# Two mixture-of-experts layers: the first pair of experts gathered alone in float32, later pairs in twos, filler products, and an output projection that ends half by half

## The chip, the cores and the metric

The kernel runs on one core of a Trainium2 chip. The metric is the device time of one execution in microseconds (us). Three executions of the kernel before took 2075.39, 2079.44 and 2080.48 us; the median, 2079.44 us, is the time before.

## The reference, cut to what matters

The program is two transformer blocks over 256 tokens of width 1024, all in float32. The first block has two sublayer pairs: a mixer (stick-breaking attention, then retention) with an output projection and a layer norm, followed by a mixture of experts (MoE) with a layer norm. Only the passage from the mixer's output projection through layer norm and router into the experts matters here:

```
h = x * (1 + scale) + shift                     # the MoE's input, x is the layer norm's output
logits = h @ router_w + router_b                # 16 experts in 4 groups
sel_group = argmax over groups of the sum of the two best probabilities
top_val, top_idx = top 2 of the logits inside that group;  top_w = softmax(top_val)
combine = sum_k one_hot(top_idx_k) * top_w_k    # 256 x 16, two entries per row
for e in range(16):
    hidden = silu(h @ w_gate[e]) * (h @ w_up[e])            # 1024 -> 512
    out += combine[:, e:e+1] * (hidden @ w_down[e])         # 512 -> 1024
```

The kernel computes only the rows that go to an expert: up to 64 rows per expert are gathered (a matrix product with a 0/1 matrix), two experts ("a pair") share one 128-wide tile, and there are eight pairs. A fallback behind a branch handles experts with more than 64 rows; it was not entered in the profiled execution.

## The kernel before, in words

Work is written as a straight program; a scheduler then orders the instructions of each engine by a simulated timeline, in program order where several are ready, so a later instruction can fill a gap that the simulation sees. `issue_after(ins)` keeps an instruction behind another on the same engine's queue.

TensorE products come in two kinds. Float32 products (`mm` on float32 tiles) are issued as two passes, so one product shows as two instructions in the trace. Products on "split" data (a high and a low part in float32r, made by `split`, line 148: a copy on ScalarE, line 151, and a subtraction on VectorE, line 153) are single passes; `mm3` multiplies high and low parts in three of them.

- `proj_out` (line 427) is the mixers' output projection. For each pair `k2` of 128-row blocks it loads a weight tile, splits it, and runs 12 products for token half t=0 and 12 for t=1.
- `layer_norm` (line 304) treats token half 0 and then half 1: two multiplies (L314), a scale-and-add with a row sum (L316), ScalarE's mean, squares and variance (L320, L324, L327), an inverse square root on GpSimd (L330), and the normalization on VectorE (L335).
- `logits` (line 554) transposes the normalized rows, copies them out of PSUM and multiplies them with the router weights (16 columns); L578 makes `r_L`. `route` (line 581) selects experts in a chain of small VectorE operations (L589 to L653). Between them stand filler products on float32 (`warm`, line 172), whose result nobody uses. Three small products give each token its slot, `pos`; `hots` (line 656) compares `pos` with a ramp to make the 0/1 matrices (L660).
- `moe` (line 664) issues weight transfers of 1 MB from SyncE's queue (L680), 96 per layer, 12 per pair. Fifteen buffers (6 `w`, 6 `hl`, 3 of the 5 `a`) hold weights. `load()` is called 14 times before the split of the normalized rows `xh` and once behind it; the fifteenth uses the buffer that `xh` leaves. `moe_rest` reads the largest expert's count into registers (L821) and branches (L822) on all engines.
- `moe_gather` (line 765) gathers two pairs at once: 32 products on the split rows, modulation on ScalarE and VectorE, then for each pair two transposes and a small product that give `m_dT` and `m_sw`, needed only when the pair's output is scattered. It is called before the loop for pairs 0 and 1, and in the loop in iterations 1, 3 and 5.
- In the loop each pair runs gate and up products (16 steps; two experts side by side on halves of the array), SiLU and a multiply (L724, L725), transposes of the hidden rows (L187), down products (8 steps), and the scatter of the pair before.

Of the kernel before, what the change touches and what calls it, by code (L numbers as in the profile page):

```python
# [15 lines left out]
OP = mybir.AluOpType  # L16
# [27 lines left out]
LAG = 2  # L44
ATR = 4
# [9 lines left out]
class Net:  # L55
# [116 lines left out]
    def warm(self, src, n=1):  # L172
# [10 lines left out]
        for _ in range(n):  # L183
            self.mm(pt, self.ones, src, True, True)

# [153 lines left out]

    def behind(self):  # L340
# [86 lines left out]
    def proj_out(self, src, o, y, first=True, last=True, between={}):  # L427

        nkb = o[0].shape[1]
        W = src.rearrange("(k p) n -> p k n", p=P)  # L430
        for k2 in range(nkb // 2):
# [4 lines left out]
            for t in range(T):  # L436
                for kk in range(2):
                    k = k2 * 2 + kk
                    oh, ol = o[0][:, k, t * P:t * P + P], o[1][:, k, t * P:t * P + P]
                    for hf in range(2):  # L440
                        cs = slice(hf * 512, hf * 512 + 512)
                        self.mm3(y[t][hf], (oh, ol), (wh[:, kk, cs], wl[:, kk, cs]),
                                 first and k == 0, last and k == nkb - 1)
# [110 lines left out]
    def logits(self, xh):  # L554
# [20 lines left out]
        while late:  # L575
            product()
        L = self.wk.tile([P, T, 16], F32, name="r_L", bufs=1)
# [3 lines left out]
    def route(self, L):  # L581
# [56 lines left out]
        self.mm(pr[:, 1], self.stri, sel[:, 1], False, True)  # L638
        cnt = self.wk.tile([P, 17], I32, name="r_cnt", bufs=1)
# [3 lines left out]
        first = self.hots(0, pos)  # L643
# [12 lines left out]
    def hots(self, pr, pos):  # L656

        dt = self.t2(512, F32R).rearrange("p (t e s) -> p t e s", t=T, e=4)
        for t in range(T):
            self.nc.vector.tensor_tensor(dt[:, t], self.iota128[:, None, :CAP].to_broadcast([P, 4, CAP]),  # L660
                                         pos[:, t, 2 * pr:2 * pr + 4, None].to_broadcast([P, 4, CAP]), op=OP.is_equal)
        return [dt[:, t].rearrange("p e s -> p (e s)") for t in range(T)]

    def moe(self, i, xh, sc, sh):
# [21 lines left out]

        hl = [self.act8(F32R).rearrange("p (t d) -> p t d", t=T) for _ in range(2)]
        for t in range(T):
            self.split(hl[0][:, t], hl[1][:, t], xh[:, t])
        xh = hl  # L690
        load()
# [14 lines left out]
        first = self.moe_gather(xh, sc, sh, hot, cmb, 0)  # L706
        self.phase(f"moe{i}")
        one = self.wk.tile([P, 1], F32, name="m_one", bufs=1)
        nc.scalar.activation(one, cmb[:, 0, 0:1], AF.Silu)
        xg, dT, sw = first.pop(0)  # L710
        nxt, late = first, None
        for pr in range(8):
# [46 lines left out]
    def modulate_slots(self, eng, out, in_, sc, sh, k):  # L759
        if eng == "s":  # L760
            self.nc.scalar.activation(out, in_, AF.Identity, scale=sc[:, k:k + 1], bias=sh[:, k:k + 1])
        else:
            self.nc.vector.tensor_scalar(out, in_, sc[:, k:k + 1], sh[:, k:k + 1], op0=OP.mult, op1=OP.add)

    def moe_gather(self, xh, sc, sh, d, cmb, pr):


        nc = self.nc
        xg = [self.t4().rearrange("p (k s) -> p k s", k=KB) for _ in range(2)]
        for k2 in range(KB // 2):  # L770
# [3 lines left out]
            for q in range(2):  # L774
                for kk in range(2):
                    k = 2 * k2 + kk
                    self.modulate_slots("vs"[k2 % 2], xg[q][:, k], pg[:, kk, q * P:q * P + P], sc, sh, k)
        out = []
        for q in range(2):
            dT = self.wk.tile([P, T, 128], F32R, name="m_dT", bufs=3)  # L780
            sw = self.wk.tile([P, 1], F32, name="m_sw", bufs=3)
            pw = self.psum()
            dq = [d[t][:, q * P:q * P + P].bitcast(F32) for t in range(T)]
# [1085 lines left out]
```

## Time and profile before

| | |
|---|---|
| time before, median of 3 | 2079.44 us (2075.39 to 2080.48) |
| profiled execution, its own time | 2080.8 us |
| its span in the trace | 2079.0 us |
| mean granted TensorE clock | 0.977 |
| busy: TensorE products, weight loads, VectorE, ScalarE, GpSimd | 95%, 74%, 59%, 39%, 20% |

The span is the stretch from the first to the last instruction of the program; 1.8 us of the execution lie around it. A matmul's end is modelled, so starts are the safer numbers; a TensorE that shows as busy is not at its peak. The two MoE layers are at about 186 to 460 us and 690 to 957 us, each from the end of the mixer's projection to the start of the next layer norm.

### The profile page before, as it was taken

The page shows a single profiled execution, that of the slowest core. Times are in us where ns is not written, and L with a number is a line of the kernel's source. Part 1 is how long each engine was busy: PE and PEld are TensorE (multiplying, and loading weights), DVE is VectorE, ACT ScalarE, POOL GpSimd, SP SyncE. Part 2 cuts the span into 40 slices and gives each one's busy share as a digit, 9 for nine tenths or more (in the row PEclk, how much of TensorE's full clock was granted, in tenths as well). Part 3 has the DMA queues.
Part 4 walks back from the last instruction along what each step waited for, and adds up shares of the span by engine and source line. Part 5 has one row for each costly group of instructions (what it writes and reads, how often), then busy time and mean ns, then how long its engine had stood idle before and what let it go on. Part 6 is the DMA issues. An engine that isn't in the chain of part 4 may idle for free.

```text
span 2079.0 us, 31873 instructions
## 1 busy us (share of the span) xinstructions
PE 1970.1 (95%) x12566; PEld 1531.0 (74%) x12567; DVE 1218.3 (59%) x2489; ACT 801.3 (39%) x1254; POOL 417.7 (20%) x319
## 2 busy tenths in 40 slices
PE   6999999989999999997888999999999999999998
PEld 4977443339998844335766889999999998888886
DVE  3645321128885422115587569767999986555555
ACT  3444111124454211113333544555444444444444
POOL 1000000002332000000231144544665550000000
PEclk8999999999999899998998999999999999999999
DMA  9797799997875699996332361544554445555554
GB/s 388 270 407 269 293 395 392 395 384 252 312 266 178 241 370 394 396 391 257 132 132 72 131 238 35 161 151 143 171 193 145 153 153 191 186 190 192 189 189 149
DMA packets 155888, 496.09 MB, mean 239 GB/s; under 512 B 10177, under 2 KB 10593, under 8 KB 147153
## 3 DMA queue, kind: packets, MB, share of 16 engines
q1 hardware_dynamic: 152880, 483.42, 64.6%
q0 software_dynamic: 2848, 10.53, 1.4%
q8 instruction: 102, 1.67, 0.3%
q14 instruction: 58, 0.47, 0.1%
HBM read 486.30 MB, written 7.61 MB: 238 GB/s over the span
## 4 chain that ended last, share of the span: by engine, by line
PE 76%; DVE 8%; ACT 2%; issue 2%; DMA 1%; POOL 1%; POOLq 0%; SPq 0%; DVEq 0%; ACTq 0%
PE ps L163 45%; PE y L163 28%; PE y L1200 1%; PE ps L187 1%; DMA w<-moe_w_down 1%; DVE pair L1547 1%; DVE hl L153 1%; DVE et L1471 1%; DVE i L1448 0%; ACT hl L151 0%; POOL hl L160 0%; DVE ps L1193 0%; DVE pos L1459 0%; DVE v L1447 0%; DVE t L725 0%
## 5 line engine op out<-in xcount | busy, mean ns | idle before, releaser
L163 PE MATMUL ps<-hn,pair 128*128 128x256 f32 x3072 | 383.3, 285 | 4.2 <-DVE pair L1547 4.1
L163 PEld LDWEIGHTS ps<-hn,pair 128*128 128x128 f32 x3072 | 373.8, 192 | 5.4 <-DVE pair L1547 4.9
L163 PE MATMUL ps<-w,t 128*64 128x512 f32 x624 | 278.9, 598 | 7.7 <-ACT t L196 2.7
L163 PE MATMUL ps<-hl,t 128*64 128x512 f32 x624 | 279.7, 599 | 4.5 <-DVE t L194 3.1
L1547 POOL TENSOR_TENSOR pair<-raw,pair 128x640 fp32r<-128x640 f32 x128 | 235.9, 1851 | 157.0 <-ACT pair L1545 150.8
L151 ACT CAST hl<-w 128x2048 fp32r<-128x2048 f32 x79 | 150.4, 1903 | 137.0 <-PE ps L163 81.3
L153 DVE TENSOR_TENSOR pair<-raw,pair 128x1024 fp32r<-128x1024 f32 x128 | 156.8, 1225 | 67.2 <-ACT pair L151 67.2
L163 PE MATMUL y<-pair,tmp 128*128 128x512 f32 x768 | 189.7, 395 | 0.0
L163 PE MATMUL y<-pair,eT 128*128 128x512 f32 x768 | 186.5, 391 | 0.0
L163 PEld LDWEIGHTS y<-pair,tmp 128*128 128x128 f32 x768 | 144.4, 188 | 33.9
L163 PEld LDWEIGHTS ps<-w,t 128*64 128x64 f32 x624 | 82.4, 137 | 117.2 <-issue 106.8
L163 PEld LDWEIGHTS y<-pair,eT 128*128 128x128 f32 x768 | 144.2, 188 | 32.4
L1545 ACT CAST pair<-raw 128x1024 fp32r<-128x1024 f32 x128 | 134.2, 1051 | 65.1 <-PE ps L163 24.6
L153 DVE TENSOR_TENSOR hl<-w,hl 128x2048 fp32r<-128x2048 f32 x51 | 118.2, 2318 | 52.8 <-ACT hl L151 49.2
L151 ACT CAST pair<-raw 128x1024 fp32r<-128x1024 f32 x128 | 133.8, 1045 | 1.1 <-issue 1.1
L163 PEld LDWEIGHTS ps<-hl,t 128*64 128x64 f32 x624 | 81.6, 137 | 68.8 <-issue 62.1
L163 PE MATMUL ps<-hl,a 128*128 128x256 f32 x1008 | 130.3, 287 | 1.8 <-ACT hl L151 1.8
L330 POOL TENSOR_TENSOR ln_st<-ln_st,c_mhalf 128x1 f32<-128x1 f32 x8 | 7.9, 982 | 604.0 <-ACT ln_st L327 604.0
L163 PEld LDWEIGHTS ps<-hl,a 128*128 128x128 f32 x1008 | 124.0, 191 | 6.1 <-ACT hl L151 2.0
L725 DVE TENSOR_TENSOR t<-t,ps 128x512 f32<-128x512 f32 x16 | 11.0, 688 | 171.5 <-PE ps L163 171.5
L163 PEld LDWEIGHTS ps<-a,hl 128*128 128x128 f32 x864 | 106.4, 195 | 3.5 <-issue 1.6
L163 PE MATMUL ps<-a,hl 128*128 128x256 f32 x864 | 108.6, 287 | 0.3 <-DVE a L153 0.3
(427 smaller groups left out, 3012.5 us busy)
## 6 DMA issues: line engine op xcount, KB each, us to landing
raw<-peer_u SPq DMA_DIRECT2D x128, 512.0 KB, 3.5
raw<-peer_v SPq DMA_DIRECT2D x128, 512.0 KB, 3.3
w<-ada_w SPq DMA_DIRECT2D x35, 1024.0 KB, 8.3
w<-moe_w_down SPq DMA_DIRECT2D x28, 1024.0 KB, 14.3
hl<-moe_w_down SPq DMA_DIRECT2D x28, 1024.0 KB, 14.2
w<-moe_w_up SPq DMA_DIRECT2D x26, 1024.0 KB, 14.3
hl<-moe_w_up SPq DMA_DIRECT2D x26, 1024.0 KB, 14.3
w<-moe_w_gate SPq DMA_DIRECT2D x24, 1024.0 KB, 14.4
```

What stands on the lines that cost most here:

```text
L151: nc.scalar.copy(hi, src)
L153: nc.vector.tensor_tensor(lo, src, hi.bitcast(F32), op=OP.subtract)
L163: self.last_mm = self.nc.tensor.matmul(out, lhsT=lhsT, rhs=rhs, start=start, stop=stop, skip_group_check=True)
L187: self.nc.tensor.transpose(out, in_, self.ident[:in_.shape[0], :in_.shape[0]])
L330: nc.gpsimd.tensor_tensor(st[:, 3:4], st[:, 2:3], self.mhalf[:, 0:1], op=OP.pow)
L725: nc.vector.tensor_tensor(hid, hid, pu, op=OP.mult)
L1200: self.nc.tensor.matmul(py[32 * q:32 * q + 32, :S], lhsT=self.s5_ct[ct][:, 4 * i + q], rhs=ab[q % 2][:, x, ri], start=j == 0, stop=j == 3, ...
L1471: V.tensor_reduce(et[:, 0:2, h], oh.rearrange("p a k j -> p a j k"), axis=AX.X, op=OP.add)
L1545: nc.scalar.copy(up[:, 0], ur)
L1547: lo = eng.tensor_tensor(up[:, 1, ks], ur[:, ks], up[:, 0, ks].bitcast(F32), op=OP.subtract)
```

## The change

The parts, in the order in which they run:

1. `proj_out`: in a last call (`last`), the second-last block pair's weights are held, and the last two pairs are multiplied together: 24 products for half 0, then 24 for half 1.
2. `logits` gets three filler products behind its last product, `route` five behind the `pos` products.
3. `hots` makes 0/1 matrices of a chosen number of experts and type: two experts in float32 for the first pair, before it was four in float32r. The register load of the count is put behind it on VectorE's queue.
4. The split of `xh` and the fifteenth `load()` move from in front of `route` to behind the first pair's gather.
5. `first_gather` gathers pair 0 alone with 16 float32 products from the unsplit `xh`. Its `m_dT` and `m_sw` (`moe_slots`) are made behind the gate and up products of pair 0.
6. Later gathers run in iterations 0, 2, 4 (pairs 1-2, 3-4, 5-6) and 6 (pair 7; its 32 products still cover two pairs' columns, and one pair's are used).
7. The fallback behind the branch gathers from the unsplit rows too.

```diff
+FILL = {"L": 3, "pos": 5}
+GATHER = {0: (1, (0, 1)), 2: (3, (0, 1)), 4: (5, (0, 1)), 6: (6, (1,))}
...
+    def fill(self, src, n):
+        with self.tc.issue_after(self.last_mm.ins):
+            self.warm(src, n)
...
 proj_out:
+            for kk in range(2):
+                held[k2 * 2 + kk] = wh[:, kk], wl[:, kk]
+            if not (last and k2 == nkb // 2 - 2):
+                for t in range(T):
+                    with self.tc.issue_after(self.last_mm.ins) if t and len(held) > 2 else nullcontext():
+                        for k, (h, l) in held.items():
...
+                                self.mm3(y[t][hf], (oh, ol), (h[:, cs], l[:, cs]),
+                                         first and k == 0, last and k == nkb - 1)
+                held = {}
...
 logits:
+        self.fill(h.rearrange("p k s -> p (k s)"), FILL["L"])
 route:
+        self.fill(self.ones, FILL["pos"])
...
-        first = self.hots(0, pos)
+        first = self.hots(0, pos, 2, F32)
...
 moe:
-        for t in range(T):
-            self.split(hl[0][:, t], hl[1][:, t], xh[:, t])
-        xh = hl
-        load()
         cmb, pos, cnt, hot = self.route(L)
...
-        first = self.moe_gather(xh, sc, sh, hot, cmb, 0)
+        xg, got = self.first_gather(xh, sc, sh, hot)
+        with self.after(*got):
+            for t in range(T):
+                self.split(hl[0][:, t], hl[1][:, t], xh[:, t], 512)
+        xh, nxt, late = hl, [], None
+        load()
         for pr in range(8):
...
+            if pr == 0:
+                dT, sw = self.moe_slots(hot, cmb, 0)
             hid = self.t2()
...
-            if pr % 2 and pr + 1 < 8:
-                nxt = self.moe_gather(xh, sc, sh, self.hots(pr + 1, pos), cmb, pr + 1)
+            if pr in GATHER:
+                b, qs = GATHER[pr]
+                nxt = self.moe_gather(xh, sc, sh, self.hots(b, pos), cmb, b, qs)
...
+    def first_gather(self, x, sc, sh, d):
+        xg, last = self.t4().rearrange("p (k s) -> p k s", k=KB), [None, None]
+        for half in range(2):
+            pg = self.psum((P, 4, P))
+            for kk in range(4):
+                k = half * 4 + kk
+                for t in range(T):
+                    self.mm(pg[:, kk], x[:, t, k * P:k * P + P], d[t], t == 0, t == 1)
+            for kk in range(4):
+                k = half * 4 + kk
+                last[kk % 2] = self.modulate_slots("sv"[kk % 2], xg[:, k], pg[:, kk], sc, sh, k)
+        return xg, last
...
 moe_rest:
-        most = nc.values_load(cnt[0:1, 16:17], min_val=0, max_val=S)
+        with self.tc.issue_after(self.hot.ins):
+            most = nc.values_load(cnt[0:1, 16:17], min_val=0, max_val=S)
```

## Rows read from the trace of the kernel before

**Rows 1.** The page, part 4: the chain that ended last, by engine.

```profile
PE 76%; DVE 8%; ACT 2%; issue 2%; DMA 1%; POOL 1%; POOLq 0%; SPq 0%; DVEq 0%; ACTq 0%
```

**Rows 2.** Windows: stretch, length, busy us per engine, clock, DMA share, GB/s.

```profile
226.00:441.00 215.00, 204.93 (x966) 87.58 (x964) 39.21 (x82) 29.29 (x58) 0.00 (x0) 0.99 1.04 393
```

**Rows 3.** Waits of TensorE, second layer's loop: total us, times, longest.

```profile
PE ps L163 <- DMA w<-moe_w_down: 1.4, 2, 0.7
```

**Rows 4.** Timeline of SyncE's queue: start, us, transfer; first layer.

```profile
205.15 0.37 SPq L680 DMA_DIRECT2D a<-moe_w_gate  x1
224.37 0.38 SPq L680 DMA_DIRECT2D w<-moe_w_gate  x1
```

**Rows 5.** Timeline, first layer's loop: down products' neighbours in pairs 0 and 7.

```profile
235.53 0.66 PE L187 MATMUL ps<-c_pack,t 128*128 128x128 f32 x4 [0.89 <-DVE t L725]
...
444.63 0.64 PE L163 MATMUL ps<-w,t 128*64 128x512 f32 x1 [0.68 <-ACT t L196]
```

**Rows 6.** Timeline, first MoE's layer norm: start, us, engine, [idle before].

```profile
192.12 1.30 DVE L314 TENSOR_TENSOR a<-y,t 128x512 f32<-128x512 f32 x2 [6.49 <-PE y L163]
...
194.77 1.37 DVE L314 TENSOR_TENSOR a<-y,t 128x512 f32<-128x512 f32 x2
...
197.87 0.81 DVE L335 TENSOR_SCALAR a<-a,ln_st 128x1024 f32<-128x1024 f32 x1 [0.38 <-POOL ln_st L330]
198.73 0.19 ACT L324 ACTIVATION_READ_ACCUMULATOR t<-a,ln_st 128x1 f32 x1
...
198.83 1.03 ACT L151 CAST a<-a 128x1024 fp32r<-128x1024 f32 x1
...
199.76 0.29 ACT L327 ACTIVATE ln_st<-ln_st,c_eps 128x1 f32<-128x1 f32 x1
...
200.13 1.54 POOL L330 TENSOR_TENSOR ln_st<-ln_st,c_mhalf 128x1 f32<-128x1 f32 x1 [2.29 <-ACT ln_st L327]
```

**Rows 7.** Timeline, a later layer norm: the same GpSimd operation.

```profile
462.39 0.55 POOL L330 TENSOR_TENSOR ln_st<-ln_st,c_mhalf 128x1 f32<-128x1 f32 x1 [252.29 <-ACT ln_st L327]
```

**Rows 8.** Timeline, first layer: fillers, slot products, gather, first expert product.

```profile
206.26 0.94 PE L163 MATMUL ps<-r_L,c_ones 128*128 128x128 f32 x6 [0.28 <-DVE r_L L578]
...
211.71 0.37 PE L163 MATMUL ps<-r_sel,c_pack 128*128 128x16 f32 x2
...
213.18 0.47 PE L163 MATMUL ps<-t,a 128*128 128x256 f32 x2 [1.09 <-DVE t L660]
...
219.41 0.38 PE L187 MATMUL ps<-c_pack,t 128*128 128x128 f32 x2
...
220.69 0.64 PE L163 MATMUL ps<-w,t 128*64 128x512 f32 x1
```

**Rows 9.** Timeline, second layer: normalization, transposes, router products, gather, first expert product.

```profile
702.54 0.81 DVE L335 TENSOR_SCALAR a<-a,ln_st 128x1024 f32<-128x1024 f32 x1 [0.44 <-POOL ln_st L330]
...
704.70 1.95 PE L187 MATMUL ps<-c_pack,a 128*128 128x128 f32 x8
...
706.58 3.60 PE L163 MATMUL y<-r_W,t 128*128 128x16 f32 x16
...
718.17 5.55 PE L163 MATMUL ps<-t,a 128*128 128x256 f32 x32 [1.05 <-DVE t L660]
...
724.83 0.64 PE L163 MATMUL ps<-w,t 128*64 128x512 f32 x1
```

**Rows 10.** Windows around router and gather, columns as in rows 2.

```profile
213.90:217.30 3.40, 3.18 (x13) 2.89 (x14) 0.43 (x1) 0.00 (x0) 0.00 (x0) 0.50 0.02 7
...
702.00:715.60 13.60, 13.31 (x59) 12.11 (x59) 7.39 (x40) 4.51 (x6) 0.51 (x1) 0.50 0.83 316
```

**Rows 11.** Timeline of TensorE, first layer, iteration 1: the gather.

```profile
259.46 3.12 PE L163 MATMUL ps<-t,a 128*128 128x256 f32 x24
262.42 0.62 PE L163 MATMUL y<-t,m_dT 128*128 128x512 f32 x2
```

More of the change, by code (lines that the diff above doesn't have):

```diff
@@ L338, in layer_norm, with after @@
         return xh
+    def after(self, *ops):
+        stack = ExitStack()
+        for op in ops:
+            stack.enter_context(self.tc.issue_after(op.ins))
+        return stack
     def behind(self):
@@ L435, in proj_out @@
             self.split(wh, wl, w)
-            for t in range(T):
[L437 to L443, printed above, removed]
+            for kk in range(2):
[4 more added lines that the diff above has]
+                        for k, (h, l) in held.items():
+                            oh, ol = o[0][:, k, t * P:t * P + P], o[1][:, k, t * P:t * P + P]
+                            for hf in range(2):
+                                cs = slice(hf * 512, hf * 512 + 512)
+                                self.mm3(y[t][hf], (oh, ol), (h[:, cs], l[:, cs]),
+                                         first and k == 0, last and k == nkb - 1)
+                held = {}
             self.background(self.rate)
@@ L687, in moe @@
         hl = [self.act8(F32R).rearrange("p (t d) -> p t d", t=T) for _ in range(2)]
-        for t in range(T):
-            self.split(hl[0][:, t], hl[1][:, t], xh[:, t])
-        xh = hl
-        load()
         cmb, pos, cnt, hot = self.route(L)
@@ L760, in modulate_slots, with moe_gather @@
         if eng == "s":
[L761 to L769, printed above, removed]
+            return self.nc.scalar.activation(out, in_, AF.Identity, scale=sc[:, k:k + 1], bias=sh[:, k:k + 1])
+        return self.nc.vector.tensor_scalar(out, in_, sc[:, k:k + 1], sh[:, k:k + 1], op0=OP.mult, op1=OP.add)
+    def first_gather(self, x, sc, sh, d):
[10 more added lines that the diff above has]
+        return xg, last
+    def moe_gather(self, xh, sc, sh, d, cmb, pr, qs=(0, 1)):
+        xg = [self.t4().rearrange("p (k s) -> p k s", k=KB) for _ in qs]
         for k2 in range(KB // 2):
@@ L773, in moe_gather, with moe_slots @@
                 self.picked(pg[:, kk], xh, 2 * k2 + kk, d)
[L774 removed]
+            for j, q in enumerate(qs):
                 for kk in range(2):
                     k = 2 * k2 + kk
[L777 to L783, printed above, removed]
[L784 to L794 removed]
+                    self.modulate_slots("vs"[k2 % 2], xg[j][:, k], pg[:, kk, q * P:q * P + P], sc, sh, k)
+        return [(x, *self.moe_slots([a[:, q * P:q * P + P] for a in d], cmb, pr + q)) for x, q in zip(xg, qs)]
+    def moe_slots(self, d, cmb, pr):
+        dT = self.wk.tile([P, T, 128], F32R, name="m_dT", bufs=3)
+        sw = self.wk.tile([P, 1], F32, name="m_sw", bufs=3)
+        pw = self.psum()
+        d = [a if a.dtype == F32 else a.bitcast(F32) for a in d]
+        for t in range(T):
+            self.transpose(pw[:, t * P:t * P + P], d[t])
+        for t in range(T):
+            self.mm(pw[:, 2 * P:2 * P + 2], d[t], cmb[:, t, 2 * pr:2 * pr + 2], t == 0, t == 1)
+        self.evac(dT, pw[:, :2 * P].rearrange("p (t s) -> p t s", t=T))
+        for e in range(2):
+            r = slice(64 * e, 64 * e + 64)
+            self.nc.vector.tensor_copy(sw[r], pw[r, 2 * P + e:2 * P + e + 1])
+        return dT, sw
     def rest_gather(self, xh, sc, sh, d, w, xg, dT, ps):
@@ L801, in rest_gather @@
             for kk in range(4):
-                self.picked(pg[:, kk], xh, half * 4 + kk, d)
+                k = half * 4 + kk
+                for t in range(T):
+                    self.mm(pg[:, kk], xh[:, t, k * P:k * P + P], d[t], t == 0, t == 1)
             for kk in range(4):
@@ L827, in moe_rest @@
             xg, ye = self.t4(), hh
[L828 removed]
+            dr = self.t2(S)
             d = [dr[:, t * P:t * P + P] for t in range(T)]
```

27 lines of the change are left out of this document (7 added, 20 removed).

## The prediction

> **What bounds the kernel now.** I began with the chain on the page: three quarters of the time ends on TensorE [rows 1]. Then I asked for windows, because the change touches only the two passages from a mixer into an MoE layer. Inside an expert loop two limits run side by side: the transfers deliver 393 GB/s at a full DMA share from start to end, and TensorE is busy 205 of 215 us [rows 2]. Which one ends last is seen where weights are used. In the first layer the last down products wait for ScalarE's copy and not for a transfer; in the second TensorE waits for down weights, 1.4 us in all [rows 3, 5]. So the first layer is TensorE's, and in the second both limits touch.
>
> SyncE's queue shows a hole that TensorE sets. The fifteenth transfer goes out at 205.15, the sixteenth at 224.37, 3.7 us behind the first expert product at 220.69, since it needs a buffer that this product reads [rows 4, 8]. So an earlier first product brings TensorE's loop and the transfers forward alike. I call that moment T1 (220.69 and 724.83) [rows 8, 9]; the change is worth what it takes from T1, less what it adds to the loop behind it.
>
> **The change, part by part, per layer (first / second).**
>
> *Projection in halves, and the split moved.* Half 1's products end when they did, and its layer norm sets the chain; only half 0 comes earlier, by another 12 products: the halves are 194.77 - 192.12 = 2.65 us apart today and 5.3 after [rows 6]. That by itself gives nothing. What gives is the split's going: ScalarE's cast of half 0 (198.83, 1.03 us) keeps half 1's variance step until 199.76, though its sum was out at 198.92: 0.8 us [rows 6]. GpSimd's inverse root then took 1.54, and 0.55 in a later layer norm with VectorE idle [rows 6, 7]; of this 1.0 I count 0.4, since VectorE has other steps to do beside it. Against this, half 0 needs 197.87 - 192.12 = 5.75 us from first multiply to normalization, so this normalization (0.81) now falls into the middle of half 1's steps on VectorE and can push them by its length [rows 6]. I take -0.4, bounds -1.8 and +0.8, in both layers. In the second, half 1's rows were ready at 702.54 + 0.81 = 703.35, but its transposes started at 704.70, because TensorE was still at half 0's router products; those now come earlier: -1.1, bounds -1.35 and 0 [rows 9].
>
> [...]
>
> *Three fillers behind the router products* cost nothing while the route's chain runs on VectorE for the 5.5 us behind them (206.26 to 211.71) [rows 8]. At half clock a group of six passes takes 6 x 0.244 = 1.5 us, by the transposes' 1.95/8, on a queue that is then late [rows 9]. I take 0, bounds 0 and +1.5.
>
> *Five fillers behind the slot products.* Ten passes at 0.94/6 = 0.157 us stand between the last slot product (211.71 + 0.37 = 212.08) and the gather: 213.65, where the gather began at 213.18 [rows 8]. The branch stands behind them on TensorE's queue; from slot products to gather it now takes 1.1 us, and if that starts only behind the fillers, the gather begins near 214.7. I take +0.6, bounds 0 and +1.5. The register load put behind `hots` binds VectorE alone, which then has nothing to do until the gather's first results: 0.
>
> *First gather.* It took 219.41 - 213.18 = 6.2 us, and 5.55 in the second layer; of the first, 3.4 us ran at a clock of 0.50 [rows 8 to 10]. The new one has 16 float32 products, 32 passes of 128 columns. The fillers are of the same form, 0.157 each with their group's modelled tail: 5.0 us, back to back somewhat less; at half clock 32 x 0.244 = 7.8 [rows 8, 9]. I take 4.4, by the filler row, at full clock: -1.8 / -1.1; bounds 4.0 and 7.8, so -2.2 to +1.6 and -1.5 to +2.3. It is no shorter in work than the old one: 24 products on split rows take 262.42 - 259.46 = 2.96 us at full clock, so 32 take 3.95 [rows 11].
>
> *Slot matrices behind the gate and up products.* In front of T1 two groups took 220.69 - 219.41 = 1.3 us, in the second layer 724.83 - (718.17 + 5.55) = 1.1 [rows 8, 9]: -1.3 / -1.1.
>
> So T1 comes earlier by 0.4 - 0.6 + 1.8 + 1.3 = 2.9 us / 0.4 + 1.1 - 0.6 + 1.1 + 1.1 = 3.1 us.
>
> *The loop* now holds four gathers where it held three, since pairs 1 and 2 are gathered in iteration 0: +3.95 [rows 11]. It makes all eight slot groups instead of six, at 1.3/2: +1.3 [rows 8]. In iteration 0 this fills the wait for the hidden rows that is idle today: -0.9 [rows 5]. The other iterations swap places (1, 3, 5 lose their filling, 2, 4, 6 gain it): 0. Sum +4.3; bounds +2.5 (two more such waits filled) and +5.5 (nothing filled).
>
> *Transfers.* The fifteenth transfer needs the buffer of the unsplit rows, now read until the split behind the gather ends: a modulation, two casts of 1.03 and a subtraction of like length, some 4.4 us behind T1, where the sixteenth goes out at T1 + 3.7 today [rows 4, 6, 8]. So the stream restarts 0.7 us later against T1 and has one more megabyte (1.05 MB at 393 GB/s, 2.7 us): +3.4 against T1 [rows 2]. TensorE's own +4.3 covers it at the end of both loops: 0, bounds 0 and +2 in the second layer, where nothing is spare. The weights held for the projection's last step delay two prefetches by 2.7 us, which fall into the hole before T1: 0.
>
> *The third projection*, into the second block, has the same order, and half 1 ends it too: 0, bounds -0.5 and +0.5.
>
> Sum: first layer 4.3 - 2.9 = +1.4; second 4.3 - 3.1 = +1.2. On the profiled execution, 2080.8 us (span 2079.0 and 1.8 around it), that is 2083.4. This execution lay 1.4 us above the median of the three runs, so the forecast is **2082**: no change that can be told (a measurement of this kernel tells some 0.3%, 6.2 us). Its own range is 2077 to 2085.
>
> **The rivals.**
>
> *The fillers hold the clock, and the loop swallows the gather (faster).* Today the second passage runs 13.6 us at half clock from 702.0 on [rows 10]. At full speed its router products would take 1.8 us less (half of 3.60), the transposes 1.0 less [rows 9]. The gather at 4.0 gives 0.4 more in each layer, fillers that take only idle time give back 0.6 twice, half 0's normalization out of the way 0.8 twice, and the loop at +2.5 instead of +4.3 gives 1.8 twice. Together 2.8 + 7.2 = 10: 2072. For it: the slow stretches came behind router and slot products of 16 columns, and the fillers go there. Against it: the lull between the halves' router products grows by the 2.7 us that half 0 is earlier, and no filler stands in it.
>
> *The float32 gather lands at half clock (slower).* One mechanism: its 32 passes cost 7.8 instead of 4.4 us in front of T1 in both layers, +6.8: 2089. It decides once 4 of these come true, when over half of both gathers runs slowly. For it: more than half of the first layer's gather does so today [rows 8, 10]. Against it: the fillers directly ahead.
>
> *The weights come too late.* The gather in iteration 0 delays the release of pair 0's down weights by some 4 us. The nine transfers then under way last 9 x 2.7 = 24 us from about T1 + 6, and a release near T1 + 28 just meets their end. If it misses by 2 us, the second layer pays that with its +3.4: 2 to 4 us over the sum, 2084 to 2086.
>
> *Part of it does nothing:* the early half 0 is the plainest case; it stands at 0 in the sum already.
>
> **How the numbers follow.** Forecast 0.47, all within 0.3%. Weights late 0.14: 0.12 within, 0.02 slower. Clock held 0.24: 0.20 faster, 0.04 within. Gather at half clock 0.15, slower. So faster 0.20, within 0.63, slower 0.17. The range reaches to both clock cases: 2071 to 2089.
>
> **What would show it.** The new gather's 32 passes in 4 to 5 us at clock 1.00; T1 about 3 us earlier against the end of the projection; the loop, from T1 to the next layer norm, longer by about 4 us in both layers, with a gather between up and down products of iteration 0; the fifteenth transfer behind the split's last subtraction. The forecast is wrong if the loop is not longer (then some 6 us faster), if the passes cost 0.24 each, or if TensorE waits for weights for more than 3 us in a layer.

## The result, and the profile after

The changed kernel is slower. Six runs gave 2095.99 us (median; 2093.45 to 2099.04), six of the kernel before beside them 2077.57 us (2071.14 to 2080.48): ratio 1.0089, with an interval of 1.0075 to 1.0104, some 18.4 us. That lies outside my range of 2071 to 2089. The profiled execution took 2095.9 us (span 2094.1), 15.1 us more than the one before. From milestones in both traces, where those 15.1 us lie (one execution of each, so a difference of 1 or 2 us in a row, and of more in the last, can be chance):

| passage | before, us | after, us | difference |
|---|---|---|---|
| start to half 1's layer norm, first layer | 194.77 | 193.20 | -1.6 |
| from there to the router's logits, first / second layer | 11.24 / 14.58 | 12.78 / 15.46 | +1.5 / +0.9 |
| logits to the first expert product (T1) | 14.68 / 14.62 | 16.61 / 17.11 | +1.9 / +2.5 |
| expert loop, T1 to its last expert product | 230.49 / 231.10 | 233.16 / 234.29 | +2.7 / +3.2 |
| last expert product of the first layer to half 1's layer norm behind retention | 244.46 | 249.28 | +4.8 |
| second loop's last expert product to the end | 1123.1 | 1122.3 | -0.9 |

T1 was to come 3 us earlier in each layer. Against the logits it comes 1.9 and 2.5 us later: 0.8 and 0.4 up to the last slot product, 3.3 and 3.4 from there to the gather; the gather itself and what stands behind it give back 2.1 and 1.3. The timeline of TensorE and its neighbours, first layer, against [rows 8] (start, duration, engine, operation, idle time before it and what ended that):

```profile
212.70 1.36 PE L165 MATMUL ps<-c_ones 128*128 128x128 f32 x10
213.33 0.49 DVE L682 TENSOR_TENSOR t<-c_pack,r_pos 128x128 f32<-128x128 f32 x2
217.22 5.44 PE L165 MATMUL ps<-t,a 128*128 128x128 f32 x32 [3.15 <-PEq L862]
221.13 0.46 ACT L786 ACTIVATE t<-ps,ada_sh,ada_sc 128x128 f32<-128x128 f32 x1 [9.44 <-PE ps L165]
222.58 0.64 PE L165 MATMUL ps<-w,t 128*64 128x512 f32 x1
```

The fillers end at 214.06, the 0/1 matrices at 213.82, and the gather starts at 217.22. For 3.15 us TensorE waits for nothing but its own sequencer (PEq), at the branch (L862). Such an idle time of 2.5 us or more ahead of a gather is called the stretch from here on. The second layer shows the same, against [rows 9]:

```profile
732.22 5.44 PE L165 MATMUL ps<-t,a 128*128 128x128 f32 x32 [3.22 <-PEq L862]
737.59 0.64 PE L165 MATMUL ps<-w,t 128*64 128x512 f32 x1
```

The windows of the two gathers, and of the passage in front of the logits (columns as in [rows 2]): the granted clock is 0.68 on average in the gathers, and 0.50 between 200.4 and 206.0, where the second half's transposes and router products ran.

```profile
217.20:222.50 5.30, 5.29 (x32) 5.26 (x32) 0.41 (x1) 0.89 (x2) 0.00 (x0) 0.68 0.01 3
732.20:737.50 5.30, 5.28 (x32) 5.27 (x32) 0.42 (x2) 0.92 (x2) 0.00 (x0) 0.68 0.01 3
200.40:206.00 5.60, 5.56 (x25) 5.23 (x26) 0.72 (x2) 1.87 (x2) 0.00 (x0) 0.50 1.04 406
```

The same place in the kernel before ran at full clock:

```profile
199.00:206.00 7.00, 6.28 (x51) 5.44 (x49) 4.46 (x5) 4.44 (x6) 1.54 (x1) 1.00 1.05 392
```

SyncE's fifteenth transfer, which went out at 205.15 before [rows 4], now stands 5.1 us behind T1, as its buffer is read until the split ends. The loop doesn't suffer: its transfers run as before [rows 2].

```profile
227.71 0.38 SPq L703 DMA_DIRECT2D a<-moe_w_gate  x1
...
228.84 0.37 SPq L703 DMA_DIRECT2D w<-moe_w_gate  x1
```

```profile
240.00:441.00 201.00, 191.73 (x918) 83.52 (x919) 38.88 (x83) 29.98 (x61) 0.00 (x0) 1.00 1.04 394
```

The retention stage lies between the two expert layers, and the diff does not touch it. The longest waits of TensorE from 460 to 706 us (engine, tile and line, what it waited for: total us, times, longest):

```profile
PE ps L165 <- DVE a L323: 3.8, 1, 3.8
PE ps L165 <- ACT t L975: 3.3, 1, 3.3
PE ps L165 <- DVE t L1009: 2.9, 2, 2.7
```

The first of these has a counterpart before: 2.6 us for VectorE at 457.6, with 0.7 us more a little later. The other two are new; from 460 us on, the kernel before has no wait over 1.0 us in this stage. All waits of the stage, from the last expert product on, come to 12.9 us, and to 7.4 before. At the end of the two new ones the granted clock was 0.50, from 527.9 to 531.3 and from 630.3 to 633.7 us; over the stage it was 0.97, where it was 0.99 before:

```profile
455.75:705.03 249.28, 236.23 (x1762) 210.63 (x1759) 183.60 (x327) 112.21 (x164) 60.08 (x64) 0.97 0.73 259
```

```profile
451.18:695.63 244.45, 236.97 (x1762) 208.19 (x1759) 183.86 (x327) 111.01 (x161) 63.13 (x63) 0.99 0.73 261
```

The two new waits in the timeline. VectorE took a background split (2.29 us) ahead of the decay product that TensorE needed. ScalarE stood 4.38 us behind a table's store, with the copy that TensorE needed queued behind that:

```profile
524.16 2.29 DVE L155 TENSOR_TENSOR hl<-w,hl 128x2048 fp32r<-128x2048 f32 x1
...
527.04 0.55 DVE L1009 TENSOR_TENSOR t<-ps,t 128x384 f32<-128x384 f32 x1
```

```profile
627.55 0.63 ACT L925 ACTIVATE a<-a 128x512 f32<-128x512 f32 x1 [4.38 <-DMA s_tab<-a]
...
630.39 0.64 ACT L975 COPY t<-ps 128x256 f32<-128x256 f32 x2
```

### The profile page after: what moved, and what is told of

It is laid out like the page before. It is cut to its first block, busy times and chain, and to the rows that moved or that the text cites. A ratio compares the mean times of both kernels' runs of the same rounds, so it can differ in the third digit from the quotient of the medians.

```text
span 2094.1 us, 32081 instructions
## 1 busy us (share of the span) xinstructions
PE 1978.4 (94%) x12662; PEld 1543.9 (74%) x12663; DVE 1217.0 (58%) x2497; ACT 802.3 (38%) x1254; POOL 410.9 (20%) x319
## 4 chain that ended last, share of the span: by engine, by line
PE 52%; DVE 8%; ACT 2%; issue 2%; DMA 1%; POOL 1%; SPq 0%; POOLq 0%; ACTq 0%; DVEq 0%
PE ps L165 26%; PE y L165 24%; PE y L1240 1%; DVE pair L1587 1%; DVE i L1488 1%; DVE et L1511 1%; DVE hl L155 0%; DMA c_swap<-swap 0%; POOL hl L162 0%; DVE pos L1499 0%; DMA raw<-peer_u 0%; DVE v L1487 0%; DVE ps L1233 0%; ACT hl L153 0%; DVE big L1595 0%
```

## The experiments

Sixteen kernels ran, each beside the kernel before on the same chip. The milestones are those of the table above; the expectations of the first four runs count the retention stage from the layer norm ahead of it (235.4 us before, 245.4 after), everything else from the last expert product (244.5 and 249.3).

### What stands ahead of the gather

**Fillers or binding?** Two edits of the changed kernel, and one of the kernel before.

```diff
 e1: -FILL = {"L": 3, "pos": 5}
     +FILL = {"L": 3, "pos": 0}
 e2: -        with self.tc.issue_after(self.hot.ins):
     +        with nullcontext():
              most = nc.values_load(...)
 e3 (before): +        self.fill(h..., 3)            # behind the router products
              +        self.fill(self.ones, 5)       # behind the pos products
```

> The changed kernel without the five fillers behind the slot products; every other instruction, and the order of the retention stage, stays. Theory A (the branch on TensorE's queue can only start behind the fillers, and then costs 3.2 us of idle TensorE): the gather begins within 0.7 us of the end of the 0/1 matrices, near 214 instead of 217.2 in the first layer, the first expert product comes 3 us earlier or more in each layer, and the time falls by 6 to 8 us, to about 2089. Theory B (the register load bound behind the 0/1 matrices on VectorE makes all engines' branch late): the idle stretch stays over 2.5 us, and the time moves by less than 2 us. Theory C (it is the clock: without fillers the gather runs at 0.50 from start to end): the gather lasts over 7 us and eats at least half of what the branch gives back.

> The changed kernel with the register load of the count no longer bound behind the 0/1 matrices; all other engines' queues stay as they are, only VectorE's second 0/1 matrix now stands behind its branch, as before the change. Theory A (fillers in front of TensorE's branch): TensorE's idle stretch ahead of the gather stays at 3 us, and the gather may begin up to 1 us later for the second matrix; time within 3 us of the changed kernel's. Theory B (the binding): the idle stretch falls to about 1.1 us, the first expert product comes 2 us earlier per layer, and the time falls by 4 us or more.

> The kernel before with the two groups of fillers alone added. Theory A: the gather of both layers begins some 4 us later than before (217 instead of 213.2), and the time rises by 5 to 8 us from the two passages. The order of the retention stage between the two expert layers is also another than before, though its source is not touched: if any new order costs (theory R), this stage, 235.4 us before and 245.4 in the changed kernel, is longer than 240 here too, and the whole is 2088 to 2096. If it was the projection's last step or the shifted gathers that cost the stage its 10 us (theory P), it stays at 235 to 237, and the whole is 2082 to 2086.

Without the five fillers the time was 2101.07 us (ratio 1.0116, 1.0084 to 1.0147), with the load unbound 2094.01 (1.0084, 1.0051 to 1.0117), with fillers alone 2085.91 (1.0046, 1.0025 to 1.0066). The gather of the first layer without pos fillers, then with the load unbound, then in the kernel before with fillers ("issue" is idle time in which the engine waited for nothing that the profile shows):

```profile
215.96 0.46 PE L165 MATMUL ps<-t,a 128*128 128x128 f32 x2 [1.15 <-DVE t L682]
216.60 0.58 PE L165 MATMUL ps<-t,a 128*128 128x128 f32 x1 [0.18 <-DVEq L862]
218.47 5.78 PE L165 MATMUL ps<-t,a 128*128 128x128 f32 x29 [1.29 <-issue]
```

```profile
216.71 5.36 PE L165 MATMUL ps<-t,a 128*128 128x128 f32 x32 [3.48 <-PEq L862]
```

```profile
214.88 6.05 PE L163 MATMUL ps<-t,a 128*128 128x256 f32 x32 [3.13 <-PEq L829]
```

The binding is out: unbound, the stretch is 3.48 us, and 2.60 in the second layer. With fillers the kernel before has it too, 3.13 and 2.61 us (its retention stage grows to 246.9 us, 240.6 by the expectation's count: that is theory R's, but the time lies in the range of theory P). But theory A fails: without fillers the second layer's gather still started 4.6 us behind the last slot product, and the first one stopped after three passes, by "issue". Theory C is half seen: without fillers the gathers ran at a granted 0.58 and 0.63 on average, the first over 8.0 us, 1.3 of them the stop. That this run is 5 us slower than the changed kernel isn't explained: in its profile 4.9 us more stand behind the second expert layer, where nothing in the order of the instructions differs. The kernel before has such a stop in its first layer, which I had passed over, after 9 passes. (The short one after 2 passes is another matter: VectorE's queue ended it, in the kernel before as without fillers.)

```profile
213.87 1.57 PEld L163 LDWEIGHTS ps<-t,a 128*128 128x128 f32 x7 [0.43 <-DVEq L822]
...
215.96 3.62 PE L163 MATMUL ps<-t,a 128*128 128x256 f32 x23 [0.22 <-issue]
```

Nine passes before, three with 6 passes (three fillers of two) more ahead of the branch, and a stretch ahead of the first pass with 16: the stop moves forward by as many passes as were added. That pointed to the code's place, and the DMA view has a queue for that. This is all of the changed kernel, queue and kind, packets, MB, share:

```profile
q8 instruction: 103, 1.69, 0.3%
```

16 KB a packet. From 745 to 2078 us there are 63 of them for 16,063 recorded products and weight loads of TensorE, one for every 255; in the kernel before, 63 for 15,928, one for every 253. So I read them as blocks of TensorE's code, of close to the 256 instructions that an expectation below counts with. In the changed kernel one is fetched from 214.06 to 215.43, behind the last filler, and the gather starts 1.8 us after it landed. So it is in every profile of this case: 20 of the 36 gathers have a stretch, and in each of the 20 a block set out behind the last slot product and landed 1.8 to 2.0 us ahead of the gather. That TensorE waits for such a block where the branch lands is no more than a reading of these times; what follows tests it.

**The place of the code (theory F).** Idle products of 16 columns, whose result nobody uses, are added where TensorE waits anyway. Each is two instructions, and all code behind moves by that.

```diff
 consts1: +    pt = net.psum((P, 512))
          +    for _ in range(N):                     # e5: 50, e6, e7: 90, e9: 100, e8: 16 (kernel before)
          +        net.mm(pt[:, :16], net.zerob, net.zerob[:, :16], True, True)
 layer_norm, behind retention (e7, e9):
          +        if (i, j) == (1, 0):
          +            with self.tc.issue_after(self.last_mm.ins):
          +                ...                        # 90 of the same
```

> The kernel before with 16 idle products (32 instructions) in the first microseconds and nothing else. Theory F: 32 is what the fillers of the first layer add ahead of its branch, and by count the landing of the first layer then lies outside the fetched block: an idle stretch of 3 us or more ahead of the gather, where before had 1.1, and the second layer's gather, unbroken before, stops once after some 4 products; the time rises by 2 to 5 us. If the fillers themselves were the cause (theory A), this kernel is the kernel before: 1.1 us in both layers and no difference in time.

> The changed kernel with 50 idle products (100 TensorE instructions) added in the first microseconds, where TensorE waits for its first weights; nothing else moves. Theory F (the idle stretch ahead of the gather is an instruction fetch: TensorE's code is fetched in blocks of 256 instructions, the branch jumps over some 430, and where the jump lands against the block borders decides): counted from the block fetches of the runs so far, a shift by 100 puts the landing of the second layer well inside a block that is already there, and leaves the first layer's outside. So the idle stretch of the second layer falls from 3.2 us to under 1.3 us, the first layer's stays over 3 us, and the time falls by 2 to 4 us. Theory A (the fillers in front of the branch cost it) and any theory of the clock or of VectorE's binding: both stretches stay at 3.2 us, since nothing near them changes.

> The same with 90 idle products (180 instructions). Theory F: now it is the first layer's landing that falls into a block already there, and the second layer's that does not: first layer's idle stretch under 1.3 us, first expert product there 2 to 3.5 us earlier against the router's logits; second layer's over 3 us. All other theories: both stay at 3.2 us.

> The changed kernel with 90 idle products at the start and 90 more behind the retention's output projection, where TensorE waits for the layer norm; the order of the retention stage is that of the changed kernel. Theory F: both idle stretches under 1.3 us, together 4 to 7 us off the changed kernel's time: 2088 to 2092. It also shows what the rest of the change costs without the fetch: the first expert product against the router's logits at 13 to 14 us in both layers, where the kernel before had 14.7 and 14.6.

> The changed kernel with 100 idle products at the start and 90 behind the retention's output projection: 20 instructions more than in the run with 90 and 90, where the border was found not to be crossed ahead of the branch. Theory F (block fetch): by the crossings seen so far (the last block border 25 to 50 instructions ahead of the gather in every run without a stretch) both layers now land in a fetched block: idle stretch under 1.5 us in both, first expert product at 12.5 to 14 us from the router's logits in both layers (changed kernel: 16.6 and 17.1), time 2086 to 2091. If at least one layer keeps a stretch over 3 us, counting instructions does not place the border well enough, or more than the border decides.

The kernel before, shifted by 32 instructions and with no filler near the branch, has the stretch in its first layer, and its second layer stops once after six products:

```profile
215.17 5.95 PE L163 MATMUL ps<-t,a 128*128 128x256 f32 x32 [4.62 <-PEq L822]
...
714.08 1.36 PE L163 MATMUL ps<-t,a 128*128 128x256 f32 x6 [1.05 <-DVE t L660]
717.00 5.11 PE L163 MATMUL ps<-t,a 128*128 128x256 f32 x26 [1.56 <-issue]
```

Its time is 2083.01 us (1.0018, 1.0000 to 1.0037). The time alone would hardly tell, but the stretch decides for theory F against the fillers. Mending the changed kernel by a shift proved harder. Shifted by 180, the changed kernel's first layer (first fence) lost the stretch as expected, 2091.13 us (1.0058, 1.0041 to 1.0075). With 200 and 180 both layers lost it (second fence), and T1 came 12.7 and 13.1 us behind the logits, as expected:

```profile
214.75 3.81 PE L165 MATMUL ps<-t,a 128*128 128x128 f32 x32 [0.67 <-DVEq L862]
```

```profile
216.16 3.81 PE L165 MATMUL ps<-t,a 128*128 128x128 f32 x32 [0.67 <-DVEq L867]
...
723.96 5.44 PE L165 MATMUL ps<-t,a 128*128 128x128 f32 x32 [0.45 <-PEq L867]
```

Two of the five missed on the stretch. Shifted by 100 (2095.58 us; 1.0077, 1.0055 to 1.0100) the second layer kept 4.4 us from slot product to gather, and with 90 and 90 (2094.74; 1.0067, 1.0046 to 1.0088) both layers kept 5.2 and 4.6. By my count the border then lay at the very edge of being crossed ahead of the branch; 20 instructions more did it in both layers. Up to the first branch the runs with 90 and with 90 and 90 have the same code, yet one fetched the block in time (211.5 us, 1.1 ahead of the last slot product) and the other did not: at the edge the count alone does not decide. The run with both layers mended took 2094.15 us (1.0081, 1.0050 to 1.0113) where 2086 to 2091 was expected: of 7.9 us won in front of the loops, its profiled execution lost 6.1 behind the second expert layer, in the second block, whose instructions the scheduler had put in another order there. Most of that can be chance: eleven profiled kernels share the changed kernel's order of this block, and it took them 1122.3 to 1128.0 us, the changed kernel's own profile being the shortest; with the other order it took 1128.4, and 1125.5 in the run with 90 and 90. Why the median stayed so high is open.

### The stage that nobody touched

```diff
 e4 (before): proj_out as in the change, nothing else
 e10: -GO = 2   +GO = 0      # GO picks the order in which retention's background jobs are handed over
 e11: -GO = 2   +GO = 1
 e14 (before): -GO = 2   +GO = 0
```

> The kernel before with the output projection's last step alone changed (the last two block pairs held, half 0 first). Passage into the experts: half 0's layer norm earlier by 2.7 us, half 1's transposes in the second layer earlier by about 1 us, first expert product earlier by 0 to 1.5 us per layer. Theory R (any new order of the retention stage costs): the stage between the expert layers differs from 235.4 us by more than 3 us, and the time follows it. Theory P (the held weights cost): the stage is 240 us or longer and the second mixer block longer as well. If neither, the time is 2076 to 2081.

> The changed kernel with the background jobs of the retention stage (modulation products of two later sublayers, tables) handed over in another order; the expert layers' code is the same. Theory R (the retention stage's loss is the order that the scheduler makes of the same instructions): from the first layer's last expert product to the layer norm behind retention, 249.3 us in the changed kernel and 249.3 to 250.6 in every run with its order, now differs by more than 2 us, and the two waits of TensorE (2.7 us for VectorE's decay product, 3.4 us for ScalarE's copy) are gone or elsewhere; time follows. Theory P (the stage is longer because more modulation products were pushed into it from the first expert layer): it stays within 1 us of 249.3, since their number is the same.

> The same with a third order of the jobs. Theory R: the stage has yet another length, between 241 and 251 us, with other or no waits over 2 us. Theory P: within 1 us of 249.3.

> The kernel before with the background jobs of the retention stage in the order that took 7 us off the changed kernel; everything outside that stage is in the same order as before. Theory R (the stage's length is a matter of the order that the scheduler happens to make): the stage, 244.5 us in the kernel before, differs by more than 1 us, in either direction (241 to 250), and the time with it. If the changed kernel's loss there was owed to the change itself, it stays at 244 to 245.

The projection alone: 2079.36 us (1.0009, 0.9994 to 1.0023), stage 241.3 us against 244.5. By the expectation's own count, from the layer norm ahead of it, that is 235.0 against 235.4, so it meets neither theory, and the time is the one given for that case; T1 came 3.1 us later against the logits in the first layer, at a gather of 7.8 us, where 0 to 1.5 earlier was expected, and 0.5 earlier in the second. So theory P, in the projection's form, is out. The changed kernel with jobs in order 0: 2088.39 us (1.0042, 1.0026 to 1.0058), stage 242.3 us, 7.0 less; the 3.3 us wait for ScalarE is gone:

```profile
PE ps L165 <- DVE a L323: 3.8, 1, 3.8
PE ps L165 <- DVE t L1009: 3.4, 2, 2.4
PE ps L194 <- DVE a L155: 1.0, 1, 1.0
```

All waits of the stage fell by 2.8 us, from 12.9 to 10.1. The other 4.2 of the 7.0 us lie in TensorE's busy time, and the clock is in it: 17 us of the changed kernel's stage ran at 0.50, and 10 us with order 0; at half the speed, the 7 us between them are worth an estimated 3.4 us.

With order 1: 2098.78 us (1.0102, 1.0074 to 1.0130), stage 249.0, by other waits (ScalarE 2.1 and 1.8, VectorE 0.9), so its length alone would have fitted theory P. In the kernel before, order 0 gave 243.4 us and 2079.13 us (1.0008, 0.9994 to 1.0023): no gain, and no test, since the kernel before shifted by 32, with the old order, had a stage of 243.3 us as well. What shows the order at work is all runs together. This stage took between 240.5 and 250.6 us, but kernels with one and the same order in it lie close: seven with the changed kernel's order (itself among them) 249.3 to 250.6, the kernel before and its shifted form 244.5 and 243.3, the three with the old projection and without fillers in the next section 240.5 to 241.0. TensorE's work is the same: 1759 passes are recorded in the stage, 256 of them modulation products, in the kernel before, the changed kernel and the four of this section. (That more modulation products had moved into it, the premise of theory P, was wrong.) So its length goes with the order that the scheduler makes, and an edit ahead of it can change that order.

### What is left of the change

```diff
 e12: change without the projection's part (second-last pair not held) and FILL = {"L": 0, "pos": 0}
 e13: e12 and
      -GATHER = {..., 6: (6, (1,))}
      +GATHER = {..., 6: (7, (0,))}                # pair 7's 128 columns alone
      -nxt = self.moe_gather(xh, sc, sh, self.hots(b, pos), cmb, b, qs)
      +nxt = self.moe_gather(xh, sc, sh, self.hots(b, pos, 2 * len(qs)), cmb, b, qs)
      -            self.picked(pg[:, kk], ...)
      +            self.picked(pg[:, kk, :len(qs) * P], ...)
 e15: change, GO = 0, 100 idle products at the start and 90 behind the first expert layer
 e16: e13 and 95 idle products behind retention's projection
```

> The changed kernel with the projection as before and without any filler: what is left is the first pair's gather, the moved split and the gathers in twos. Its instruction count ahead of the first branch is that of the kernel before, so by theory F the first layer's gather begins 1.1 us behind the slot products and stops once, after some 9 products, and the second layer's waits over 3 us (its branch lies 50 behind a border). The retention stage's order is near that of the kernel before: by theory R 243 to 246 us. The loops cost 2.7 and 3.2 us more than before in any theory. Sum against before: first layer 0 to +2, second +4 to +6, retention 0 to +2: 2082 to 2088. If the fillers were what held the clock, the gathers and the router products are slower here than in the changed kernel, and the time is 2092 or more.

> The run with old projection and no filler, with one edit: the last gather (pair 7 alone) works on that pair's 128 columns and not on 256. Theory W (the loops' extra time is TensorE's work for the fourth gather): the last gather's 32 products take about half of their 3.9 us, and both loops shorten by 1.5 to 2 us, from 234.2 to about 232.5; time 3 to 4 us less than that run's 2085. Theory T (the loop ends by its transfers): less than 0.5 us per loop, time unchanged.

> The changed kernel with the shorter order of the background jobs and with idle products (100 at the start, 90 behind the first expert layer) that put the landing of both branches into a fetched block. If fetch (two times 3 us and what the clock loses behind it) and order (7 us) are the loss, 18.4 us falls to 2 to 6 us: 2081 to 2086, and what is left are the loops' 6 us less what the gathers give. If it stays above 2088, there is a third cause.

> The first pair alone from unsplit rows, later pairs in twos with the last on its own columns, old projection, no filler, and 95 idle products behind the retention's projection so that the second layer's branch lands in a fetched block. By the sums so far, against the kernel before: expert products begin 2.2 us earlier in the first layer and 1.5 us in the second, loops 1.5 us longer each, retention stage 3 to 4 us shorter by its order: 2074 to 2080, no slower than the kernel before and perhaps 3 us faster. If the loops' extra time isn't the passes, 2080 to 2084.

Without fillers and projection: 2085.03 us (1.0033, 1.0019 to 1.0047); the profiled execution was the fastest of its ten, 2077.16, so the stages below don't show all of that loss. The first layer's gather began 1.25 us behind the slot products and stopped after 2 and 9 passes, the second's began after 4.5; logits to T1 12.5 and 15.7 us. Layer norm to logits took 11.2 us in both layers, at full clock and without a filler, so the fillers are not what holds the clock there. It also shows what the moved split does without the projection: half 1's normalization is early, and its transposes are not, as they start behind half 0's router products:

```profile
197.07 0.80 DVE L342 TENSOR_SCALAR a<-a,ln_st 128x1024 f32<-128x1024 f32 x1
...
199.57 1.07 PE L194 MATMUL ps<-c_pack,a 128*128 128x128 f32 x8
```

The narrow last gather shortened both loops by 0.6 us (234.2 to 233.7), 2084.35 us (1.0016, 1.0005 to 1.0027), where 1.5 to 2 and about 2081 were expected. The halved gather takes almost as long as a whole one, 0.111 us a pass and not 0.120:

```profile
398.49 3.68 PE L165 MATMUL ps<-t,a 128*128 128x128 f32 x31
```

So the size in theory W was wrong. That the loops' extra time is the gather's passes is neither shown nor refuted, since they didn't get fewer.

The changed kernel with order 0 and the shifts: **2078.70 us** (0.9999, 0.9983 to 1.0015). The whole loss is gone. The time lies below the 2081 to 2086 that was expected, although only the first layer's stretch went (2.1 us from slot product to gather; the second kept 4.1). The stage took 243.2 us, logits to T1 13.1 and 15.5. Alone, order took 10.4 us off the 18.4 and the shift by 180 took 6.2, each to some 3.5 us; together that leaves 1.8, and 0.2 was measured. That the two sum is shown to this width only: of order's 10.4 us the stage itself has 7.0. The parts that were to pay, neither layer with a stretch: 2079.38 us (1.0000, 0.9986 to 1.0013), with logits to T1 at 12.4 and 12.5 us, the stage at 240.7, loops 233.7. No version beats the kernel before.

## Why the prediction was wrong

It said 2082 us from a sum of +1.4 and +1.2. That sum is near what the change is worth with the other order and one stretch away (2078.7 against 2078.5), but that agreement is in part luck, as several terms below missed in opposite directions. Two side effects were missing from it.

- *Five fillers behind the slot products: +0.6, bounds 0 and +1.5.* **This step failed.** From the last slot product to the gather it took 1.35 / 1.32 us before and 4.63 / 4.69 after, +3.3 and +3.4. The fillers' own 1.4 us are a part of that; most is the stretch, 3.15 and 3.22 us of idle TensorE, which fell to 0.67 and 0.45 with the shifts by 200 and 180 and the fillers in place. By theory F it is the wait for the code at the branch's target. I asked what the branch has to wait for on the queue, and not where its target's code is. The row that shows it stands in the trace of before (the stop after 9 passes), right behind one that I used.
- *Everything outside the two passages: nothing.* **The missing step.** I priced the source's unchanged stages at zero. The schedule is made over the whole program, and the retention stage came out 4.8 us longer, by 5.5 us more of waits; with the same change and another order it was 7.0 shorter than that.
- *Three fillers behind the router products: 0, bounds 0 and +1.5.* Inside: from logits to the last slot product it took 5.81 / 6.64 before and 6.62 / 7.05 after. At a like clock (0.71 and 0.72) kernels without them took 5.81 and with them 6.02, so 0.2 is theirs and the rest is the clock.
- *First gather 4.4 us, by the filler row.* Mis-sized: 3.81 at full clock (1.00, in the shifted runs), just under the bound of 4.0, and 5.44 where the window has 0.68. My 0.157 us a pass carried the group's modelled tail; passes go out every 0.11. The rival of a gather at half clock had the direction right; its price, 3.4 us a layer, was three times what the change shows (5.44 against my 4.4: 1.0).
- *Slot matrices moved: -1.3 / -1.1.* Right: T1 follows the gather's last product by 0.2 us, where it took 1.4.
- *Layer norm and split: -0.4.* Right in size where the clock is full: layer norm to logits then takes 10.7 to 10.9 us in several runs (first layer of the run with the load unbound, both layers of those shifted by 100 and with order 1), against 11.24 before. But that was luck, for the reason was wrong. I gave the whole of it to the split's going and nothing to the halves. GpSimd's inverse root did fall, from 1.54 and 1.52 beside the subtraction to 0.55 with VectorE idle (198.98 and 709.59), by the whole 1.0 and not by the 0.4 that I counted. With the split moved and the old projection, half 1's normalization then starts 5.27 us into its layer norm and not 6.93, and yet the logits come only 0.05 us earlier (11.19), because TensorE is at half 0's router products until then. It takes both parts; the projection alone gave 11.09 in the second layer.
- *The clock in that passage.* The changed kernel's profiled execution, at 12.78 and 15.46, ran it largely at half clock, so the faster rival did not come. My own objection to it holds up: between half 0's router products and half 1's transposes the first layer now has a lull of 1.25 us, with three short products on zeros in it (199.04), where TensorE went straight on before. Of the eleven profiled kernels with the new projection (ten of them with the split moved) eight then ran half 1's transposes and router products wholly or partly at 0.50, with 11.2 to 13.8 us from layer norm to logits, and three at 1.00; all seven with the old one ran at 1.00. Against 11.2 with the old projection, three of the eleven gained 0.6 us, one came out even, and seven lost 1.1 to 2.6. That the lull does it is not shown, and in the second layer some kernels with the old projection are slow there too.

```profile
197.23 1.96 PE L165 MATMUL y<-r_W,t 128*128 128x16 f32 x16 [0.65 <-DVE t L201]
199.04 0.81 PE L165 MATMUL y<-c_zerob 128*128 128x512 bf16 x3
200.44 1.97 PE L194 MATMUL ps<-c_pack,a 128*128 128x128 f32 x8 [0.59 <-DVE a L342]
```

- *Second layer's transposes -1.1.* Not to be seen: what made them late before was the half clock of that one execution. The kernel before shifted by 32, same code, ran its second half's transposes in 1.09 us and the router products in 1.96, where [rows 9] have 1.95 and 3.60.
- *Loop +4.3, bounds 2.5 and 5.5* (nothing filled is 3.95 + 1.3 = 5.25). +2.7 and +3.2: inside. One gather sits between up and down products of iteration 0 as said (237.11 to 241), but the wait for the hidden rows that it fills there is back in another iteration: five such waits in the first layer, 4.3 us in all, before and after.

```profile
236.47 0.44 PE L194 MATMUL ps<-c_pack,t 128*128 128x128 f32 x2
236.74 0.51 PE L165 MATMUL ps<-r_cmb,t 128*128 128x2 f32 x4
237.11 4.08 PE L165 MATMUL ps<-t,a 128*128 128x256 f32 x32
```

- *Transfers 0; weights late 2 to 4 us.* The step held, the rival did not come: in the second loop TensorE waits for no transfer, where before it waited 1.4 us for down weights [rows 3].

## What to carry to other kernels

Behind a branch, look at the instruction fetches as at any other transfer: here 32 idle instructions in the first microseconds brought a stretch of 4.62 us to the kernel before at 215 us, and 180 took the changed kernel's 3.15 us away. A tuned kernel may owe some us to such a place. Where a scheduler orders the whole program, an edit's price includes the stages that it re-orders, so compare the orders of the unchanged stages first, and try the edit under several neutral orders before judging it. A sum of local terms can come within 2 us of what the parts are worth, here in part by luck, while the kernel moves by 18.

## What the hardware showed that I had not expected

- At a granted clock of 1.00 a TensorE pass with its own weights goes out every 0.111 us with 16 or 128 columns moved (slot products, float32 gather), and every 0.120 us with 256: half the columns buys 0.009 us.
- In the 20 gathers where a block of code set out behind the last slot product and landed ahead of the gather, TensorE was idle for 2.6 to 4.6 us, in the other 16 for 0.4 to 1.4; the block itself was under way for 1.0 to 1.9 us of that (1.36 and 1.02 in the changed kernel).
- The clock at the same place of the same code differs between executions. In the kernel before the window 702.0 to 714.8 was granted 0.50, in the same kernel shifted by 32 instructions the like window 0.82; and the gather right behind the fillers got 1.00 in the first layer of three runs and 0.68 in the second layer of one of them, both with under 0.7 us of idle before it. What sets this is open.

```profile
702.00:714.80 12.80, 12.52 (x55) 11.30 (x55) 6.66 (x36) 3.71 (x6) 0.51 (x1) 0.50 0.88 336
```

```profile
702.10:711.50 9.40, 8.77 (x58) 8.01 (x59) 6.62 (x35) 3.67 (x6) 0.52 (x1) 0.82 1.04 398
```
